# Feature-major products over 256 and 384 token columns instead of 386 and 256, with the padding columns put in where products leave PSUM

## The chip, the cores and the metric

The kernel runs on one core of a Trainium2 chip. The metric is the device time of one execution in microseconds (us). A core has five engines that run their own instruction streams and meet at semaphores: TensorE (PE, with its weight loads shown apart as PEld), VectorE (DVE), ScalarE (ACT), GpSimd (POOL) and SyncE (SP), which here issues all transfers.

## The reference

Two request groups share the weights of two trunk layers: one of 128 context tokens and one of 512 latent tokens. In each layer a combined projection feeds grouped-query attention and a bidirectional state-space scan (SSD); a depthwise convolution over three neighbouring tokens runs on the x, B and C channels and again on the up-projection of the feed-forward part. A convolution must not reach from the last context token into the first latent token, since these are two sequences.

```python
def dw_conv(x, w, b):
    width = w.shape[0]
    pad = width // 2
    xp = jnp.pad(x, ((0, 0), (pad, width - 1 - pad), (0, 0)))
    out = b
    for i in range(width):
        out = out + xp[:, i:i + seq] * w[i]
    return out

def trunk_layer(x, mod, rope, ctx_k, ctx_v, init_state, p):
    h = modulate(x, sh1, sc1)
    proj = h @ p['w_in']
    ...
    attn = block_attention(q, k_all, v_all)
    xbc = jax.nn.silu(dw_conv(xbc, p['conv_w'], p['conv_b']))
    ssd, h_final = ssd_branch(xbc, z, dt_raw, ...)
    merged = jax.nn.sigmoid(ga) * (attn @ p['w_attn_o']) + jax.nn.sigmoid(gs) * (ssd @ p['w_ssd_o'])
    x = x + g1 * (merged @ p['w_out'])
    h = modulate(x, sh2, sc2)
    u = dw_conv(h @ p['w_up'], p['ffn_conv_w'], p['ffn_conv_b'])
    u_val, u_gate = jnp.split(u, 2, axis=-1)
    x = x + g2 * ((jax.nn.silu(u_gate) * u_val) @ p['w_down'])
```

## The kernel before

**Tokens.** The 640 tokens are five tiles of 128: tile 0 is the context, tiles 1 to 4 are the latent grid. Every fp32 product is made of three matmuls on values rounded to a short form and their remainders: high by high, high by low, low by high.

**Two kinds of product.** A token-major product (`tok_major`) holds a token tile as weights and moves 512 columns of a weight matrix; 24 matmuls make one. A feature-major product (`feat_half`) holds 128 weight columns and moves tokens, which the convolution wants along the free dimension. It is done in two parts `h` of 24 matmuls each. The normalised tokens `hT` (and `h2` after the second norm) lie in four tiles, high and low for each part, in the buffers `slab0` and `slab1`.

**Padding before.** Two columns of zeros stand between the context and the latent tokens already in `hT`: `new_hT` has GpSimd set them to zero, so that part 0 has 386 columns (tiles 0 to 2 and the padding) and part 1 has 256 (tiles 3 and 4). The products carry the zeros along, and `conv_in` copies each part out of PSUM as one run of columns: once plainly into `raw`, once times the middle tap plus the bias into `cc`. `conv_taps` then adds the left and right neighbours over 642 columns. There are 69 feature-major products of two parts in each layer: 16 for x, 8 for B and C, one for dt, 44 for the up-projection.

**Order.** Nothing is issued as it is written. `Flow` records all operations with what they read and write, and a list scheduler orders them with its own costs and its own count of free buffers; each engine's program is that order. A buffer class hands its buffers out in the order in which they were asked for. The first product of `up_item` in each layer runs its part 0 for four feature tiles and then its part 1 for the four; all later ones alternate the parts. Directly ahead of it stands `w_out_item`, whose last loop normalises the token tiles one after another (`norm_tile`): VectorE adds to the residual, ScalarE sums squares, GpSimd takes the root, VectorE scales, TensorE transposes (eight matmuls against the identity, called T3 for tile 3 and T4 for tile 4 below), ScalarE and VectorE apply shift and scale, and both write the high and the low half into `h2`.

**Tokens waiting in DRAM.** `tok_load` reads attention and SSD outputs back in pieces of four feature tiles, into the same `slab0` and `slab1` buffers.

Of the kernel before, what the change touches and what calls it, by code (L numbers as in the profile page):

```python
# [7 lines left out]
F32 = mybir.dt.float32  # L8
# [10 lines left out]
P = 128  # L19
# [5 lines left out]
HALF = (386, 256)  # L25
HOFF = (0, 386)
# [14 lines left out]
def _mask(dims, cache={}):  # L41
    """Bits of the free elements that an access pattern touches."""
    m = cache.get(dims)
    if m is None:
        m = 1
        for s, n in reversed(dims):
            if s == 0 or n == 1:
                continue
            if m == 1 and s == 1:
                m = (1 << n) - 1  # L50
            else:
                b = 0
                for i in range(n):
                    b |= m << (s * i)
                m = b
        cache[dims] = m
    return m
# [22 lines left out]
class Flow:  # L80
    """Records the program as operations on tiles, orders them with a list scheduler (dependences by the
    elements touched, buffers granted in the order in which they were asked for) and issues them in that order."""
# [259 lines left out]
def hybrid_step_kernel(  # L342
# [159 lines left out]
    # token-major product: stationary tokens, moving weights of 512 columns  # L502
# [16 lines left out]
    # tokens in two parts: tiles 0 to 2 and tiles 3 and 4  # L519
    def part(i):  # L520
        return (0, col(i)) if i < 3 else (1, col(i) - HOFF[1])

# [4 lines left out]
    # tokens that wait in DRAM: two quads of feature tiles, in pieces of four, tile after tile  # L527
    def tok_load(src, q0):
        pieces = []
        tiles = []  # L530

        def load(n):
            for _ in range(n):
                i = len(tiles)
                while len(pieces) < 4 * i + 4:
                    h, k = (0, 6) if len(pieces) < 12 else (1, 4)
                    t = slab(h, [P, k, 4, P], F32R)
                    pieces.extend(t[:, j] for j in range(k))
                for r in range(2):
                    t = t2((P, 4, P))  # L540
                    dma.dma_start(t.rearrange("p k t -> p (k t)"), src[q0 + r, i])
                    split(pieces[4 * i + 2 * r], pieces[4 * i + 2 * r + 1], t)
                tiles.append(lambda a, kt, i=i: pieces[4 * i + 2 * (kt // 4) + a][:, kt % 4, :])

        return tiles, load

    # feature-major product: stationary weights of 128 columns, moving tokens
# [12 lines left out]
    def new_hT():  # L560
        res = []
        for _ in range(2):
            pair = [slab(h, [P, 8, HALF[h]], F32R) for h in range(2)]
            pool.memset(pair[0][:, :, P:P + 2].bitcast(F32), 0.0)
            res.append(pair)
        return res
# [5 lines left out]
    def norm_x(xh, xns, junk):  # L572
        """Both halves of a token tile over their root mean square."""
# [28 lines left out]
    def norm_tile(x0, x1, t, i, modT, hT):  # L602
        """x0 and t are written over."""
# [11 lines left out]
    def mw():  # L615
        """Of its own while attention holds the other buffers."""
        return t2() if flow.cls == "m" else flow.tile(tmp, [P, 512], F32, "mw", nm("mw"), 1)
# [34 lines left out]
    # the first shifts and scales, straight to features on partitions: columns of silu(cond) in two parts  # L652
    def mod_T_first(ws):
# [3 lines left out]
        for n in range(2):  # L657
            for m in range(2):
# [15 lines left out]
                # the two parts and the bias  # L674
# [30 lines left out]
    def conv_bufs():  # L705
        raw, cc = cv()[:, 0:COLS + 2], cv()[:, 0:COLS]
        pool.memset(raw[:, 0:1], 0.0)
        pool.memset(raw[:, COLS + 1:COLS + 2], 0.0)
        return raw, cc

    def conv_in(raw, cc, ps, h, w1, b):
        o = HOFF[h]
        act.activation(cc[:, o:o + HALF[h]], ps, AF.Identity, scale=w1, bias=b)
        act.copy(raw[:, 1 + o:1 + o + HALF[h]], ps)

# [11 lines left out]
    def later(fn):  # L727
        """Record what was put off last, put this off in its stead."""
# [11 lines left out]
    # ================= the program as a list of items =================  # L740
# [59 lines left out]
    def layer(l):  # L800
# [13 lines left out]
        def qk_normed(ps, n0, nh, t, a):  # L814
            """RMS norm per head, then rotary (t >= 1) or plain weights (t == 0); token-major."""
# [84 lines left out]
        def attn_gen(g):  # L900
            kT, V = S["kT"], S["V"]
            qT, qc = S["qT", g], S["qc", g]
            # context tokens
# [56 lines left out]
        def dt_item(ws):  # L960
            raw = cv()
            for h in range(2):
                ps = feat_half(ws[0], P, 0, S["hT"], h)
                act.activation(raw[0:64, HOFF[h]:HOFF[h] + HALF[h]], ps[0:64, :], AF.Identity, bias=S["dtb"])
# [69 lines left out]
        def to_tok(cc, dst):  # L1034
            """feature-major padded [128, 642] -> token-major [128 tok, 5, 128 feat]"""
# [71 lines left out]
        def ssd_gen(g):  # L1107
# [23 lines left out]
            # C over B, and B by tokens behind it, in two parts  # L1131
# [23 lines left out]
            # context states leave as they are  # L1155
# [429 lines left out]
```

## Time and profile before

| | us |
|---|---|
| three timed runs | 2855.76, 2860.41, 2860.75 |
| their median | 2860.41 |
| span of the profiled execution, first to last instruction | 2854.8 |
| TensorE busy in that span | 2816.5 |
| VectorE, ScalarE, GpSimd busy | 2066.4, 1291.9, 90.5 |

The profiled execution is listed by its span alone; its own time with what lies around the span is not among the runs, of which the fastest is 1.0 us and the median 5.6 us above the span. The trace puts all operations on one source line (the recording helper), so they are told apart by tiles and shapes. A matmul's listed duration holds its pipeline as well; what it costs in a dense stream is the distance from its start to the start of the next.

### The profile page before, as it was taken

The numbers are of one execution on the slowest core, as the hardware profiler recorded it, in microseconds if no ns is written. First come the engines' busy times: TensorE is split into PE (matmuls) and PEld (weight loads), VectorE is DVE, ScalarE is ACT, GpSimd is POOL, SyncE is SP. The second block draws the span as 40 slices with busy tenths as digits, with TensorE's granted clock in tenths as the row PEclk, the third lists the DMA queues.
The fourth block names the chain that finished last, engine by engine and source line by source line (L and its number), as shares of the span: only waits on it lengthen the run. The fifth ranks groups of instructions, "written<-read, shape, count | busy, mean of one in ns | idle before, by whom it ended". The sixth has DMA issues, their size and how long they took to land.

```text
span 2854.8 us, 41191 instructions
## 1 busy us (share of the span) xinstructions
PE 2816.5 (99%) x15620; PEld 2456.6 (86%) x15620; DVE 2066.4 (72%) x2851; ACT 1291.9 (45%) x2255; POOL 90.5 (3%) x408
## 2 busy tenths in 40 slices
PE   6999999999999999999999999999999999999999
PEld 4898997877788898998979989887887888989898
DVE  7878775987799599997677666598779456545554
ACT  6454654445353453452444645544454325524342
POOL 1200000000000000000011000000000000000000
PEclk9999999999999999999999999999999999999999
DMA  7343444677868546455352223457667553252423
GB/s 262 100 125 126 126 151 143 225 247 245 275 219 275 180 136 215 167 175 180 98 168 85 94 95 100 155 199 251 220 235 258 203 175 132 86 166 65 155 84 111
DMA packets 309679, 478.45 MB, mean 168 GB/s; under 512 B 19808, under 2 KB 139792, under 8 KB 304360
## 3 DMA queue, kind: packets, MB, share of 16 engines
q1 hardware_dynamic: 309480, 475.81, 50.0%
q8 instruction: 123, 2.02, 0.3%
q14 instruction: 76, 0.62, 0.1%
HBM read 384.08 MB, written 91.65 MB: 167 GB/s over the span
## 4 chain that ended last, share of the span: by engine, by line
PE 95%; DMA 3%; DVE 1%; ACT 1%; issue 0%; SPq 0%; POOL 0%; DVEq 0%; ACTq 0%
PE pf L178 79%; PE p L178 10%; PE pp L178 4%; PE pq L178 1%; DMA tmp<-in_state_ssd_dram 1%; DMA slab<-in_w_mod_dram 0%; DVE tmp L178 0%; DMA ga<-tmp 0%; DVE wl L178 0%; DMA tmp<-in_x_prompt_dram 0%; ACT tmp L178 0%; SPq L178 0%; DMA slab<-in_q_norm_dram 0%; DVE slab L178 0%; ACT wh L178 0%
## 5 line engine op out<-in xcount | busy, mean ns | idle before, releaser
L178 PE MATMUL pf<-wh,slab 128*128 128x512 f32 x3920 | 1268.3, 400 | 5.9 <-ACT slab L178 2.5
L178 PE MATMUL pf<-slab,wh 128*128 128x256 f32 (+1 forms) x4416 | 980.2, 311 | 3.4 <-DVE slab L178 1.9
L178 PEld LDWEIGHTS pf<-wh,slab 128*128 128x128 f32 x3920 | 733.1, 189 | 174.4 <-issue 7.3
L178 PE MATMUL pf<-wl,slab 128*128 128x512 f32 x1960 | 780.7, 398 | 0.0
L178 PEld LDWEIGHTS pf<-slab,wh 128*128 128x128 f32 x4416 | 741.8, 189 | 12.0 <-issue 5.7
L178 PE MATMUL pf<-slab,wl 128*128 128x256 f32 (+1 forms) x2208 | 685.1, 310 | 0.0
L178 DVE TENSOR_TENSOR wl<-wr,wh 128x2048 fp32r<-128x2048 f32 (+1 forms) x156 | 350.7, 2248 | 145.3 <-ACT wh L178 144.5
L178 PEld LDWEIGHTS pf<-wl,slab 128*128 128x128 f32 x1960 | 369.5, 189 | 86.6 <-issue 6.0
L178 ACT CAST wh<-wr 128x2048 fp32r<-128x2048 f32 (+1 forms) x156 | 293.0, 1879 | 320.7 <-PE pf L178 302.4
L178 PEld LDWEIGHTS pf<-slab,wl 128*128 128x128 f32 x2208 | 415.9, 188 | 3.0 <-issue 0.2
L178 DVE SCALAR_TENSOR_TENSOR tmp<-tmp,fw,tmp 128x642 f32<-128x642 f32 x176 | 155.5, 885 | 80.5 <-ACT tmp L178 66.3
L178 PE MATMUL p<-tmp,slab 128*128 128x64 f32 (+1 forms) x976 | 209.8, 336 | 0.3 <-DVE tmp L178 0.3
L178 ACT ACTIVATE tmp<-tmp 128x642 f32<-128x642 f32 (+2 forms) x176 | 120.9, 687 | 179.1 <-DVE tmp L178 145.5
L178 ACT ACTIVATE tmp<-pf,fw 128x386 f32<-128x386 f32 (+1 forms) x176 | 109.0, 620 | 175.4 <-PE pf L178 172.2
L178 DVE TENSOR_TENSOR tmp<-pf,tmp 128x512 f32<-128x512 f32 x100 | 68.3, 688 | 132.1 <-PE pf L178 131.8
L178 PEld LDWEIGHTS p<-tmp,slab 128*128 128x128 f32 x976 | 136.0, 190 | 16.2 <-ACT tmp L178 4.6
L178 ACT COPY tmp<-pf 128x256 f32<-128x256 f32 (+3 forms) x296 | 127.5, 431 | 44.1 <-PE pf L178 43.7
L178 DVE TENSOR_TENSOR slab<-tmp,slab 128x512 fp32r<-128x512 f32 (+4 forms) x182 | 109.0, 634 | 42.9 <-ACT slab L178 42.7
L178 DVE SCALAR_TENSOR_TENSOR macc<-tmp,cT,macc 128x512 f32<-128x512 f32 x196 | 137.7, 743 | 1.2 <-DMA tmp<-in_w_mod_dram 1.2
L178 DVE TENSOR_TENSOR tmp<-tmp,tmp 128x512 f32<-128x512 f32 (+3 forms) x190 | 133.7, 705 | 3.0 <-DMA tmp<-sz 0.6
L178 PEld LDWEIGHTS p<-cst,tmp 128*128 128x128 f32 (+2 forms) x750 | 92.3, 141 | 40.6 <-issue 16.1
L178 PE MATMUL p<-cst,tmp 128*128 128x128 f32 (+2 forms) x750 | 121.0, 276 | 5.1 <-DMA tmp<-in_state_ssd_dram 4.4
(131 smaller groups left out, 2564.3 us busy)
## 6 DMA issues: line engine op xcount, KB each, us to landing
wr<-in_w_in_dram SPq DMA_DIRECT2D x60, 1024.0 KB
wr<-in_w_up_dram SPq DMA_DIRECT2D x44, 1024.0 KB
slab<-row SPq DMA_DIRECT2D x40, 1024.0 KB
tmp<-in_w_mod_dram SPq DMA_DIRECT2D x116, 256.0 KB
tmp<-xres SPq DMA_DIRECT2D x85, 256.0 KB
wr<-in_w_down_dram SPq DMA_DIRECT2D x20, 1024.0 KB
tmp<-xs SPq DMA_DIRECT2D x72, 256.0 KB
xres<-tmp SPq DMA_DIRECT2D x70, 256.0 KB
```

What stands on the lines that cost most here:

```text
L178: self.ops.append((lane, lambda: call(*args, **kw), self._cost(lane, fn, outs, ins, kw), deps, touched, self.cls))
```

## The change

Part 0 becomes tiles 0 and 1 (256 columns) and part 1 tiles 2, 3 and 4 (384 columns); `hT` has no padding. `conv_in` writes a part out of PSUM tile-wise through a view (`padded`) that leaves the two padding columns out, and `conv_bufs` has GpSimd set these two columns to zero in `raw` and in `cc`. `dt_item` writes through the same view. `tok_load` follows the new sizes: the first two tiles of a quad lie in `slab0`, the other three in `slab1`. Comments were taken out as well.

```diff
-HALF = (386, 256)
-HOFF = (0, 386)
+HALF = (256, 384)
...
     def part(i):
-        return (0, col(i)) if i < 3 else (1, col(i) - HOFF[1])
+        return (0, i * P) if i < 2 else (1, (i - 2) * P)
+
+    def padded(t, b, o=0):
+
+        if b == 0:
+            return t[:, o:o + 2 * P + 4].rearrange("p (a t) -> p a t", a=2)[:, :, 0:P]
+        return t[:, o + col(2):o + COLS].rearrange("p (a t) -> p a t", a=3)
...
-                    h, k = (0, 6) if len(pieces) < 12 else (1, 4)
+                    h, k = (0, 4) if len(pieces) < 8 else (1, 6)
...
     def new_hT():
         res = []
         for _ in range(2):
-            pair = [slab(h, [P, 8, HALF[h]], F32R) for h in range(2)]
-            pool.memset(pair[0][:, :, P:P + 2].bitcast(F32), 0.0)
-            res.append(pair)
+            res.append([slab(h, [P, 8, HALF[h]], F32R) for h in range(2)])
         return res
...
     def conv_bufs():
         raw, cc = cv()[:, 0:COLS + 2], cv()[:, 0:COLS]
         pool.memset(raw[:, 0:1], 0.0)
+        pool.memset(raw[:, P + 1:P + 3], 0.0)
+        pool.memset(cc[:, P:P + 2], 0.0)
         pool.memset(raw[:, COLS + 1:COLS + 2], 0.0)
         return raw, cc
 
     def conv_in(raw, cc, ps, h, w1, b):
-        o = HOFF[h]
-        act.activation(cc[:, o:o + HALF[h]], ps, AF.Identity, scale=w1, bias=b)
-        act.copy(raw[:, 1 + o:1 + o + HALF[h]], ps)
+        ps = ps.rearrange("p (a t) -> p a t", t=P)
+        act.activation(padded(cc, h), ps, AF.Identity, scale=w1, bias=b)
+        act.copy(padded(raw, h, 1), ps)
...
-                act.activation(raw[0:64, HOFF[h]:HOFF[h] + HALF[h]], ps[0:64, :], AF.Identity, bias=S["dtb"])
+                act.activation(
+                    padded(raw[0:64], h), ps[0:64].rearrange("p (a t) -> p a t", t=P), AF.Identity, bias=S["dtb"]
+                )
```

The change also moves instructions, through the scheduler. The first place is TensorE where `w_out_item` of the second layer ends and the up-projection begins; `pf_3689` is the last product of `w_out`, `pf_3709` and `pf_3712` are the first two up products, `slab_3653` and `slab_3655` the high and low half of part 0 of `h2`. Before:

```order
L178 MATMUL pf_3689<-wh_3646,slab_3562 128x512
L178 MATMUL pf_3689<-wl_3647,slab_3560 128x512
L178 MATMUL pf_3709<-slab_3653,wh_3649 128x386
L178 MATMUL pf_3712<-slab_3653,wh_3698 128x386
L178 MATMUL pf_3709<-slab_3655,wh_3649 128x386
L178 MATMUL pf_3709<-slab_3653,wl_3650 128x386
```

and with the change:

```order
L177 MATMUL pf_3689<-wh_3646,slab_3562 128x512
L177 MATMUL pf_3689<-wl_3647,slab_3560 128x512
L177 MATMUL pf_3709<-slab_3653,wh_3649 128x256
L177 MATMUL pf_3709<-slab_3655,wh_3649 128x256
L177 MATMUL pf_3709<-slab_3653,wl_3650 128x256
L177 MATMUL pf_3709<-slab_3653,wh_3649 128x256
```

The second up product's first matmul no longer stands between a high and a low matmul of the first one. Some hundred rows further, the transposes of tile 4 (T4, `p_3591` and `p_3592`) and the first matmul of part 1 (`pf_3719`, from `slab_3654` and `slab_3656`) stand in the changed kernel as follows, with 95 matmuls of 256 columns between the end of `w_out` and T4:

```order
L177 MATMUL pf_3718<-slab_3653,wh_3698 128x256
L177 MATMUL pf_3718<-slab_3655,wh_3698 128x256
L177 MATMUL p_3591_3695<-cst_84,tmp_3692 128x128 x4
L177 MATMUL p_3592_3696<-cst_84,tmp_3691 128x128 x4
L177 MATMUL pf_3718<-slab_3653,wl_3699 128x256
L177 MATMUL pf_3719<-slab_3654,wh_3649 128x384
L177 MATMUL pf_3719<-slab_3656,wh_3649 128x384
```

Before, T4 stood earlier in the part, inside the third product, and 45 matmuls of part 0 followed it:

```order
L178 MATMUL pf_3715<-slab_3653,wl_3650 128x386
L178 MATMUL p_3591_3695<-cst_84,tmp_3692 128x128 x4
L178 MATMUL p_3592_3696<-cst_84,tmp_3691 128x128 x4
L178 MATMUL pf_3715<-slab_3653,wh_3649 128x386
L178 MATMUL pf_3715<-slab_3655,wh_3649 128x386
```

The second place is ScalarE in the same stretch: `tmp_3707` and `tmp_3708` are `raw` and `cc` of the first up product, `tmp_3684` and `slab_3654` belong to tile 3, `tmp_3692`, `tmp_3691` and `sm_3693` to tile 4. Before:

```order
L178 CAST wh_3701<-wr_3700 128x2048
L178 ACTIVATE tmp_3684<-p_3583_3687,sm_3627 128x128 x4
L178 CAST slab_3654<-tmp_3684 128x4x128
L178 ACTIVATE tmp_3708<-pf_3709,fw_2252 128x386
L178 ACTIVATE tmp_3691,sm_3693<-tmp_3692 128x512
L178 COPY tmp_3707<-pf_3709 128x386
L178 ACTIVATE tmp_3691,sm_3693<-tmp_3690 128x512
```

and with the change:

```order
L177 CAST wh_3701<-wr_3700 128x2048
L177 COPY tmp_3707<-pf_3709 128x2x128
L177 ACTIVATE tmp_3708<-pf_3709,fw_2252 128x2x128
L177 ACTIVATE tmp_3684<-p_3583_3687,sm_3627 128x128 x4
L177 CAST slab_3654<-tmp_3684 128x4x128
L177 ACTIVATE tmp_3691,sm_3693<-tmp_3692 128x512
L177 COPY tmp_3710<-pf_3712 128x2x128
L177 ACTIVATE tmp_3691,sm_3693<-tmp_3690 128x512
```

Both copies of the first up product now stand ahead of tile 3's shift and scale, and a copy of the second one stands between the two sums of squares of tile 4.

## Rows read from the trace of the kernel before

**Rows 1.** The page, part 1: busy time and share of each engine.
```profile
PE 2816.5 (99%) x15620; PEld 2456.6 (86%) x15620; DVE 2066.4 (72%) x2851; ACT 1291.9 (45%) x2255; POOL 90.5 (3%) x408
```

**Rows 2.** Waits of TensorE: us in total, times, longest.
```profile
PE p L178 <- DMA tmp<-in_state_ssd_dram: 4.4, 5, 1.4
...
PE pf L178 <- ACT slab L178: 3.9, 4, 1.6
PE pf L178 <- DVE slab L178: 3.9, 4, 1.7
```

**Rows 3.** Groups by shape, TensorE: count, then busy us and mean ns.
```profile
L178 PE MATMUL pf<-slab,wh 128*128 128x386 f32 x2208 | 585.3, 343 | 3.4 <-DVE slab L178 1.9 <-ACT slab L178 1.5
...
L178 PE MATMUL pf<-slab,wl 128*128 128x386 f32 x1104 | 377.0, 341 | 0.0
```

**Rows 4.** Timeline of TensorE, up-projection of layer 2: start, duration (us).
```profile
2466.20 0.52 PE L178 MATMUL pf<-slab,wh 128*128 128x386 f32 x2
...
2470.46 0.40 PE L178 MATMUL pf<-slab,wh 128*128 128x256 f32 x2
...
2473.19 0.52 PE L178 MATMUL pf<-slab,wh 128*128 128x386 f32 x2
```

**Rows 5.** Timeline of TensorE inside `w_out` of layer 2.
```profile
2374.54 0.64 PE L178 MATMUL pf<-wh,slab 128*128 128x512 f32 x2
...
2380.10 0.62 PE L178 MATMUL pf<-wh,slab 128*128 128x512 f32 x2
```

**Rows 6.** Timeline of TensorE in attention, layer 1.
```profile
160.38 1.04 PE L178 MATMUL pp<-slab,slab 128*128 128x320 f32 x6
161.26 0.33 PE L178 MATMUL pf<-slab,wh 128*128 128x386 f32 x1
```

**Rows 7.** Timeline of TensorE, `w_out` to up-projection, layer 2; idle in brackets.
```profile
2383.51 0.39 PE L178 MATMUL pf<-wl,slab 128*128 128x512 f32 x1
2384.64 0.59 PE L178 MATMUL pf<-slab,wh 128*128 128x386 f32 x2 [0.74 <-ACT slab L178]
2386.18 0.42 PE L178 MATMUL pf<-slab,wh 128*128 128x386 f32 x1 [0.94 <-DVE slab L178]
...
2389.20 1.43 PE L178 MATMUL p<-cst,tmp 128*128 128x128 f32 x8
...
2397.55 1.06 PE L178 MATMUL p<-cst,tmp 128*128 128x128 f32 x8
```

**Rows 8.** Timeline of TensorE at the same place in layer 1.
```profile
979.80 0.59 PE L178 MATMUL pf<-slab,wh 128*128 128x386 f32 x2 [0.73 <-ACT slab L178]
981.34 0.41 PE L178 MATMUL pf<-slab,wh 128*128 128x386 f32 x1 [0.95 <-DVE slab L178]
...
983.34 1.09 PE L178 MATMUL p<-cst,tmp 128*128 128x128 f32 x8
```

**Rows 9.** Windows: stretch, length, busy us by engine, PEclk, DMA share.
```profile
978.00:981.50 3.50, 1.81 (x8) 1.04 (x7) 3.50 (x5) 3.50 (x9) 0.63 (x1) 1.00 0.03 13
...
2386.60:2390.40 3.80, 3.80 (x18) 3.70 (x17) 3.40 (x6) 1.01 (x2) 0.90 (x5) 0.55 0.96 341
```

**Rows 10.** Timeline of VectorE, layer 2: scaling of tile 3, a weight remainder.
```profile
2387.63 0.89 DVE L178 TENSOR_SCALAR tmp<-tmp,sm 128x512 f32<-128x512 f32 x2 [0.40 <-POOL sm L178]
...
2389.03 2.29 DVE L178 TENSOR_TENSOR wl<-wr,wh 128x2048 fp32r<-128x2048 f32 x1
```

**Rows 11.** Timeline of ScalarE, layer 2: shift and scale, then high halves.
```profile
2398.21 1.51 ACT L178 ACTIVATE tmp<-p,sm 128x128 f32<-128x128 f32 x4
2399.76 1.14 ACT L178 CAST slab<-tmp 128x512 fp32r<-128x512 f32 x2
```

**Rows 12.** Timeline of VectorE, layer 2: low halves of tile 4.
```profile
2400.41 1.29 DVE L178 TENSOR_TENSOR slab<-tmp,slab 128x512 fp32r<-128x512 f32 x2 [0.39 <-ACT slab L178]
```

**Rows 13.** Groups by shape, ScalarE's scaled copy of 256 columns, GpSimd memsets.
```profile
L178 ACT ACTIVATE tmp<-pf,fw 128x256 f32<-128x256 f32 x88 | 49.6, 564 | 53.2 <-PE pf L178 53.2
...
L178 POOL MEMSET tmp<- 128x1 f32 x272 | 18.1, 107 | 1156.0 <-DVE tmp L178 766.0 <-DMA xs<-tmp 83.3 <-DMA xres<-tmp 82.8
```

## The prediction

> **What bounds the kernel now.** The page's first part comes first: TensorE is busy for 2816.5 of 2854.8 us, no other engine for more than 72% [rows 1]. Then the waits of TensorE: the reader should see how short the list is. The waits for SSD states, for the high halves (ScalarE) and for the low halves (VectorE) of feature-major operands come to 4.4, 3.9 and 3.9 us [rows 2]; half of the latter two are the two places where `w_out` hands over to the up-projection [rows 7, 8]. So the time is the number of TensorE's matmuls times their distance in a dense stream, plus a few us of stalls. What frees ScalarE, VectorE or GpSimd is worth nothing by itself; what shortens a matmul counts in full, what makes TensorE wait counts too.
>
> **The distance of matmuls.** The listed durations of some 340 ns [rows 3] hold the pipeline, so distances are read from starts. One part of 386 columns takes from 2466.20 to 2470.46 us for 24 matmuls, 177.5 ns each, and the following part of 256 columns to 2473.19, 113.8 ns each [rows 4]. In `w_out` 24 matmuls of 512 columns take 5.56 us, 231.7 ns each [rows 5]; in attention six of 320 take 0.88 us, 146.7 ns each [rows 6].
>
> **The two columns.** The change makes no matmul fewer; it makes 386 columns into 384 in 2208 + 1104 = 3312 matmuls [rows 3]. No row shows 384 columns. From 256 to 386 a column costs 63.7/130 = 0.49 ns, from 386 to 512 it costs 54.2/126 = 0.43 ns. Two columns are then 0.86 to 0.98 ns; I take 0.92, and 3312 x 0.92 ns = **3.0 us**. The upper bound comes from straight lines that leave 386 out, in case it is an awkward size. Between 320 and 512 a column costs 85.0/192 = 0.443 ns, so 384 would take 146.7 + 28.3 = 175.0 ns, 2.5 ns less than 386: 8.3 us in all. Between 256 and 512 it would take 113.8 + 128 x 0.461 = 172.7 ns, 4.8 ns less: 15.9 us. A loss I exclude, since fewer columns are streamed from the same buffers. I take the low end, because 386 is the nearest row, and because 320, which is as round as 384, also lies above the line from 256 to 512 (143.3 ns there, 146.7 measured).
>
> **The hand-over to the up-projection.** Here the change moves a wait, and this needs a chain of its own for each layer.
>
> Before, part 0 needs tile 2, the third of five. In layer 2 the last `w_out` matmul starts at 2383.51, so a dense stream would go on at 2383.74; the first high matmul starts at 2384.64 and the first low one two matmuls later, at 2386.18, 1.18 us later than it might. That is 2.0 us lost [rows 7], and the same in layer 1 [rows 8]. In layer 2 the granted clock then falls to 0.55 for 3.8 us, mostly its lower level, 1.2 GHz [rows 9], and T3 takes 1.43 us where it took 1.09 in layer 1 [rows 7, 8]. From 2386.6 to T3 at 2389.20 eight matmuls start, about 320 ns apart; against 177.5 this loses 1.2 us, with T3 1.5 us. So this place costs 2.0 us in layer 1 and 3.5 us in layer 2: **5.5 us**.
>
> After, part 0 needs tiles 0 and 1 alone, which are long done; both stalls go. What is late next is tile 4, since part 1 now needs tiles 2 to 4, and four parts of 256 columns cover less than four of 386 did. In layer 2: T3 stands 38 matmuls behind 2383.74, at 2388.1, and its operand is scaled from 2387.63 on, half of it in 0.45 us [rows 10]: 0.1 us of waiting at most. T4 comes after 95 matmuls (10.8 us) and T3 (0.9): 2395.4. Its operand hangs on ScalarE, where the copies of the first product, at most 0.57 us each [rows 13], now stand ahead of tile 3's shift and scale, and where a copy of the second product stands between tile 4's two sums of squares. That copy waits for a buffer which VectorE frees with tile 3's first low half, after a weight remainder that ends at 2391.3 [rows 10], so about 2392.2. I reckon the squares end at 2393.5, the root and the scaling's first half at 2395.8 (estimate by the same steps before): 0.4 us of waiting. From T4's start to tile 4's first high half it took from 2397.55 to 2400.3, to its first low half until 2401.05, that is 2.8 and 3.5 us [rows 7, 11, 12], while T4 and the one matmul behind it fill 1.0 us. TensorE waits 1.9 us, runs one high matmul and waits 0.5 more. Sum: about 2.9 us, and the chance of one in two (one of the two gaps of 2 us did it) of the same clock loss of 1.5 us: 3.6, against 3.5 before. In layer 1 six matmuls of the modulation fill part of the gap once T4's PSUM tile is read; I reckon 1.5 us there against 2.0. Net gain **0.5 us**, bounds: both stalls vanish (5.5 us gained), or both are 2 us longer than reckoned and the clock falls twice (about 6 us lost).
>
> The Trainium skill's page TensorE: Matmul & The Clock Gate, section What's actually happening, says that the monitor's window runs free and doesn't start with the kernel; so the same gap may cost clock in one place and not in another. The trace agrees: of two equal gaps only one was followed by a clock of 0.55 [rows 9]. By this rule the repeated runs of one kernel differ at such a place too.
>
> **The memsets.** GpSimd gets 272 memsets of two columns and loses eight on `hT`: 264 x 107 ns [rows 13] is 28 us on an engine busy for 90.5 [rows 1], and none is on TensorE's chain in the up-projection, where `conv_taps` starts a whole part later. Were the cover gone, VectorE would start its taps 0.1 to 0.4 us later per product, and with a busy share of 72% it takes that up. The Trainium skill's page SBUF — State Buffer, section Who interferes with whom, speaks against them: GpSimd and VectorE share a port pair, and a VectorE operation in a two-port mode blocks or is blocked in full while the other runs. The page counts tensor_scalar among these, which scales the tiles here. At each hand-over some seven of these memsets lie near tile 4's chain; at 107 ns each [rows 13] that would be 0.7 us twice, and the gain of the hand-over would turn into a loss of 0.9 us. No row shows such a block, so the sum leaves it out and the range holds it.
>
> **What else moves.** ScalarE copies the same columns in parts of 256 and 384; a strided write could cost it more, and it is busy for 45% [rows 1]. The token quads come back one tile later into `slab1`: a tile that was split during three later products (3 x 5.56 us [rows 5]) now has two, 11 us, for two casts and two subtractions of 0.57 and 0.65 us [rows 11, 12]. Hidden. The order of attention and SSD between the feature-major products shifts by a product here and there; TensorE waits there for states in five places [rows 2], and this may go either way by 1 to 2 us.
>
> **Sum.** 2854.8 - 3.0 - 0.5 = 2851.3 us of span. Against the median of the runs shown, 5.6 us above the span of the profiled execution: 2860.4 - 3.5 = **2856.9 us**, 0.12% faster. About 0.2%, 5.7 us, is what a measurement of this kernel can tell from no change.
>
> **Rivals.**
> 1. *384 is a better size than the neighbour shows.* For it: 386 lies 1.7 to 4.8 ns above the lines through rounder sizes. Against it: 320 lies above the line from 256 too. It gives 8.3 + 0.5 = 8.8 us, 2851.6 us, and as far as 2844 by the other line.
> 2. *The hand-over eats the gain.* Part 1 waits for tile 4 as reckoned and the clock falls in both layers: stalls of 2.9 + 1.5 + 2 x 1.5 = 7.4 us against 5.5. With the columns: -3.0 + 1.9, 2859.3 us. For it: the gap is again over 2 us long. Against it: in layer 1 other matmuls split it.
> 3. *Slower: the states come late.* The new order in SSD brings the transposes of the states ahead of their transfers. There are sixteen such loads (two layers, four groups, two directions); five wait now, up to 1.4 us [rows 2]. Eleven more at 1.4 us are 15.4 us: 2872.3 us. It decides, that is ends over 0.2% slower, from seven more at 1.4 us (9.8 against 3.5 gained). Against it: five of sixteen wait now, and the program moves by a product at most places.
>
> **Chances.** The likeliest, two columns at the price of their neighbours and waits that trade places: 0.58, with its own range of 2852 to 2861 (hand-over 3 us either way, runs scattering). Rival 1: 0.20. Rival 2: 0.12. Rival 3: 0.08. Something else: 0.02. The range that leaves out the far ends of rivals 1 and 3 is 2849 to 2864 us. Faster by over 0.2%: a fifth of the likeliest and most of rival 1, 0.29. Slower: rival 3 and little else, 0.08. Within: 0.63.
>
> **What would show it.** In the profile after: 24 matmuls of 384 columns take 4.24 us (176.6 ns each) where rival 1 has 4.20 or less; those of 256 stay at 113.8. At the end of `w_out` TensorE goes straight into 256-column matmuls, in both layers, and the bracketed waits for ScalarE and VectorE stand at the first 384-column product behind T4, of about 1.9 and 0.5 us in layer 2. The waits for states stay near 4 us. The prediction is wrong if 384 columns take under 175 ns, if the wait behind T4 is over 4 us or gone, or if a new wait shows in attention or SSD.

## The result and the profile after

| | us |
|---|---|
| four timed runs of the changed kernel | 2880.12 to 2881.49 |
| their median | 2880.43 |
| median of the kernel before | 2860.45 |
| ratio, with its 95% interval | 1.0081 (1.0067 to 1.0095) |
| span of the profiled execution | 2879.7 |

The changed kernel is 0.8% slower; 2856.9 us was predicted. The profiled executions differ by 24.9 us, since that of before lies at the lower end of its runs; against the medians 20 us are to be explained.

The page of the changed kernel, part 1, answers to [rows 1]: the same number of matmuls, 9.5 us more busy time of TensorE, and so some 15 us more in which it doesn't run.

```profile
PE 2826.0 (98%) x15620; PEld 2459.2 (85%) x15620; DVE 2067.5 (72%) x2851; ACT 1293.1 (45%) x2255; POOL 110.4 (4%) x672
```

The waits of TensorE (us in total, times, longest) answer to [rows 2]. The waits for states went down, and a wait for a VectorE result that had a row of 1.5 us before leads the list.

```profile
PE pf L177 <- DVE tmp L177: 12.2, 3, 10.5
...
PE p L177 <- DMA tmp<-in_state_ssd_dram: 1.6, 1, 1.6
```

Where that is, the stages tell. In each layer the z and gate products are followed by the attention's output product (`attn_o`), by that of the SSD in two halves of its channels (`ssd_oA` and `ssd_oB`, ten products each) and by `w_out`. Last matmuls of each stage of layer 1 against before: gates 0.9 us earlier, `ssd_oA` 862.04 against 859.97, `ssd_oB` 943.43 against 919.05. So 22 of the 24.9 us come up between the ends of `ssd_oA` and `ssd_oB` of layer 1, and after that the two kernels stay 20 to 26 us apart to the end. The timeline of TensorE there, with idle time in brackets:

```profile
867.88 0.72 PE L177 MATMUL pp<-tmp,slab 128*128 128x512 f32 x2
...
880.32 1.67 PE L177 MATMUL p<-tmp,slab 128*128 128x64 f32 x14
...
887.68 0.39 PE L177 MATMUL pf<-wl,slab 128*128 128x512 f32 x1
898.57 1.22 PE L177 MATMUL pf<-wh,slab 128*128 128x512 f32 x2 [10.50 <-DVE tmp L177]
```

The `pp` and 64-column matmuls are the SSD's last two token tiles; before, they stood ahead of the end of `ssd_oA`, and from 860 us on TensorE ran nothing but products and transposes. Now they are late: `ssd_oB` needs the SSD's output, and when the few products that can run without its last tile are done, TensorE has nothing left. The same stretch in windows (busy us by engine, then PEclk, DMA share, GB/s) shows VectorE full while TensorE is empty, and the granted clock at 0.63, that is mostly at its lower level of 1.2 GHz. From 898.5 to 905 us it is 0.66, which costs some 2 us more (an estimate, 6.5 x 0.34):

```profile
890.00:900.00 10.00, 1.44 (x3) 1.16 (x4) 10.00 (x17) 0.62 (x1) 0.00 (x0) 0.63 0.92 322
```

The 22 us are not all waiting. Between these two ends TensorE is idle for 11.2 us in gaps of over 150 ns, where it had none before; its products take 2.7 us longer, 10.2 us of the stretch being at the lower clock; and 8.3 us are matmuls of the SSD and transposes that had been done by then before. So the nearly equal ends of `ssd_oA` hide some 10 us (8.3 + 2.1) that TensorE had lost already: up to there its gaps come to 29.8 us against 25.7, and the clock was at the lower level for 17.1 us against 10.2.

What the last tile waits for stands in SyncE's queue and on VectorE. `y<-tmp` stores an SSD output tile and `tmp<-y` brings it back; of eight loads of modulation weights six are queued ahead of the last store and two between it and its return:

```profile
884.49 2.90 SPq L177 DMA_DIRECT2D tmp<-in_w_mod_dram  x6
887.49 0.60 SPq L177 DMA_DIRECT2D y<-tmp  x1
890.05 1.65 SPq L177 DMA_DIRECT2D tmp<-in_w_mod_dram  x2
893.47 0.33 SPq L177 DMA_DIRECT2D tmp<-y  x1
```

and on VectorE the modulation sums stand ahead of the tile's low half and of the addition that empties a PSUM buffer (`tmp<-pf,tmp`):

```profile
889.94 7.37 DVE L177 SCALAR_TENSOR_TENSOR macc<-tmp,cT,macc 128x512 f32<-128x512 f32 x11
897.23 0.68 DVE L177 TENSOR_TENSOR slab<-tmp,slab 128x512 fp32r<-128x512 f32 x1
897.83 0.68 DVE L177 TENSOR_TENSOR tmp<-pf,tmp 128x512 f32<-128x512 f32 x1
```

Before, the last store was this one, 29 us earlier and 1.6 us ahead of the last matmul of `ssd_oA`:

```profile
858.34 0.38 SPq L178 DMA_DIRECT2D y<-tmp  x1
```

The lag has a history. The products up to `ssd_oA` end within 6 us of where they ended before, but attention's last store goes from 452.95 to 471.57 us, the first SSD store from 529.39 to 544.19, the eleventh from 707.35 to 737.83. In layer 2 the SSD is some 26 to 37 us later than before too, of which 24 are layer 1's; there its last store, at 2247.28, is 42 us ahead of the end of `ssd_oA`, so it costs nothing.

**Distances.** In the up-projection of layer 2, 24 matmuls of 256 columns now take 2.83 us, 117.9 ns each, and 24 of 384 take 4.16 us, 173.3 ns each; it was 113.8 for 256 and 177.5 for 386 [rows 4]:

```profile
2756.05 0.40 PE L177 MATMUL pf<-slab,wh 128*128 128x256 f32 x2
...
2758.88 0.51 PE L177 MATMUL pf<-slab,wh 128*128 128x384 f32 x2
...
2763.04 0.40 PE L177 MATMUL pf<-slab,wh 128*128 128x256 f32 x2
```

The two parts together take what they took, 6.99 us. For the accounts below I use means over all starts of a trace (start to next start inside the products, gaps left out):

| ns from start to start | before | changed |
|---|---|---|
| 386 / 384 columns, up-projection (2112 matmuls) | 177.4 | 173.3 |
| 386 / 384 columns, x, B, C and dt (1200) | 177.1 | 173.4 |
| 256 columns, up-projection (2112) | 113.7 | 117.7 |
| 256 columns, x, B, C and dt (1200) | 116.7 | 117.4 |
| 512 columns, all token-major products (5880) | 231.8 | 232.8 |

That is 8.5 + 4.5 = 13.0 us less, 8.3 + 0.8 = 9.1 us more and 6.0 us more: a dense stream that is 2.1 us longer. The 512-column rise has a place: products whose weights are token tiles from `slab0` and `slab1` (k, v, q, z, gates, `attn_o`, `ssd_oA`, `ssd_oB`: 85 of them in each layer, 4080 matmuls in all) go from 231.5 to 233.1, while `w_out` and the down-projection, with weights from other buffers, stay between 231 and 232.5.

**The hand-over** in layer 2 [rows 7]: TensorE goes straight from `w_out` into part 0 at 2408.33, and waits behind tile 4's transposes instead.

```profile
2420.47 1.04 PE L177 MATMUL p<-cst,tmp 128*128 128x128 f32 x8
...
2423.31 0.44 PE L177 MATMUL pf<-slab,wh 128*128 128x384 f32 x1 [1.69 <-ACT slab L177]
...
2424.04 0.45 PE L177 MATMUL pf<-slab,wh 128*128 128x384 f32 x1 [0.29 <-DVE slab L177]
```

Behind these waits the granted clock falls in layer 2 as it did before: it is 0.63 from 2424.0 to 2428.6 us, mostly the lower level; in layer 1 it stays at 1.00. From the end of `w_out` to the end of the up-projection the changed kernel gains 1.5 us on before in layer 1 and nothing in layer 2.

### The profile page after: what moved, and what is told of

Same layout as the page of the kernel before. It is cut to its first block, busy times and chain, and to the rows that moved or that the text cites. A ratio compares the mean times of both kernels' runs of the same rounds, so it can differ in the third digit from the quotient of the medians.

```text
span 2879.7 us, 41481 instructions
## 1 busy us (share of the span) xinstructions
PE 2826.0 (98%) x15620; PEld 2459.2 (85%) x15620; DVE 2067.5 (72%) x2851; ACT 1293.1 (45%) x2255; POOL 110.4 (4%) x672
## 4 chain that ended last, share of the span: by engine, by line
PE 95%; DMA 2%; DVE 1%; ACT 1%; issue 1%; SPq 0%; POOL 0%; DVEq 0%; ACTq 0%; POOLq 0%
PE pf L177 79%; PE p L177 10%; PE pp L177 4%; PE pq L177 1%; ACT tmp L177 1%; DVE tmp L177 1%; DMA slab<-in_w_mod_dram 0%; DMA tmp<-in_x_prompt_dram 0%; DMA tmp<-in_state_ssd_dram 0%; DVE wl L177 0%; DMA slab<-row 0%; DVE slab L177 0%; SPq L177 0%; DMA slab<-in_q_norm_dram 0%; POOL sm L177 0%
## 5 line engine op out<-in xcount | busy, mean ns | idle before, releaser
L177 PE MATMUL pf<-slab,wh 128*128 128x384 f32 (+1 forms) x4416 | 980.0, 310 | 2.3 <-ACT slab L177 1.7
L177 PE MATMUL pf<-slab,wl 128*128 128x384 f32 (+1 forms) x2208 | 684.7, 310 | 0.0
L177 ACT ACTIVATE tmp<-pf,fw 128x384 f32<-128x384 f32 (+1 forms) x176 | 108.9, 619 | 177.1 <-PE pf L177 168.9
L177 ACT COPY tmp<-pf 128x384 f32<-128x384 f32 (+3 forms) x296 | 127.5, 431 | 36.7 <-PE pf L177 35.0
L177 DVE SCALAR_TENSOR_TENSOR tmp<-tmp,tmp 128x642 f32<-128x642 f32 (+2 forms) x130 | 98.2, 757 | 42.8 <-ACT tmp L177 41.9
L177 ACT CAST slab<-tmp 128x512 fp32r<-128x512 f32 (+2 forms) x146 | 91.6, 650 | 74.0 <-DVE tmp L177 42.6
```

The costliest lines, as they stand in the source:

```text
L177: self.ops.append((lane, lambda: call(*args, **kw), self._cost(lane, fn, outs, ins, kw), deps, touched, self.cls))
```

## Experiments

**Is it the order, or the parts themselves?** Four kernels. Two are the kernel before with one number of its scheduler changed, two are the changed kernel. First:

```diff
-                    heapq.heappush(slots[x.tag], x.end + 150.0)
+                    heapq.heappush(slots[x.tag], x.end + 151.0)
```

> The kernel before with one number of its scheduler changed: a buffer is reckoned free 151 ns after its last use instead of 150. The same operations on the same tiles; only the order in which they stand can differ. In that order the SSD's last output tile of layer 1 stands about five 512-column products later beside the products. Theory A (the loss of the change is the order: SSD work falls behind the products, and at the end of ssd_oA in layer 1 TensorE has no product left): the last store of an SSD output tile in layer 1 goes from 858 us to about 880 to 888, TensorE waits 8 to 12 us between ssd_oA and ssd_oB, and the time is 2872 to 2884 us. Theory B (the parts of 256 and 384 columns, their copies or their loads cost the time wherever they stand): 2860 us, plus or minus 3, since none of them is in this kernel.

Measured: 2872.97 us (before, on the same chip: 2858.54), ratio 1.0051 (1.0036 to 1.0066). The last store is at 878.37, and TensorE waits at the same place, without a single part regrouped. Its products are 6.4 us earlier than before at the end of `ssd_oA` and 14.9 us later at the end of `ssd_oB`:

```profile
889.77 1.22 PE L178 MATMUL pf<-wh,slab 128*128 128x512 f32 x2 [10.11 <-DVE tmp L178]
```

The same line with 152.0:

> The kernel before with the same number at 152 ns. The order differs from that of before too, but the SSD's last tile of layer 1 stands as early as before. Theory A: last store at 858 us plus or minus 4, no wait of over 2 us between ssd_oA and ssd_oB, 2857 to 2864 us. Theory B: the same, 2860 us. A rival to theory A, that any disturbance of an order that was picked out costs some 20 us, expects 2870 us or more here.

Measured: 2859.11 us, ratio 0.9999 (0.9990 to 1.0009); last store at 858.25. So it isn't that any nudge costs: of 150, 151 and 152 only 151 does.

Third, the changed kernel with another price of a matmul:

```diff
-                return max(n, 256) / 2.4 + 2 if n > 128 else 213.0
+                return max(n, 256) / 2.4 + 4 if n > 128 else 213.0
```

> The changed kernel, its scheduler reckoning a matmul at its columns at full clock plus 4 ns instead of 2. The operations are those of the changed kernel; in their order the SSD's last tile of layer 1 stands before the end of ssd_oA, as it did before the change. Theory A: no wait of over 3 us between ssd_oA and ssd_oB, the whole 24 us of that stretch come back but for 2 or 3: 2855 to 2862 us. Theory B: only the wait itself goes (10.5 us and some 2.5 us of lower clock behind it), and the rest stays: 2866 us or more.

Measured: 2869.58 us, ratio 1.0046 (1.0030 to 1.0063): by its number that is theory B. The trace speaks for A in this stretch: last store at 853.17, no wait, and at the end of `ssd_oB` of layer 1 the kernel is level with before (919.09 against 919.05). Its 11 us are lost in layer 2, from the gates on, where this order has a new wait in `attn_o`, with the lower clock around it:

```profile
2156.12 1.19 PE L177 MATMUL pf<-wh,slab 128*128 128x512 f32 x2 [3.17 <-DVE tmp L177]
```

Fourth, the side work in front of the tile is held back:

```diff
+                    if i == 3 and n == 0:
+                        S["oB"].append(len(flow.ops) - 1)
...
+                if held:
+                    flow.hold = held[0]
...
-            mod_item(0, 10)
-            mod_item(0, 11)
+            mod_item(0, 10, S["oB"])
+            mod_item(0, 11, S["oB"])
```

> The changed kernel with the loads of the last two modulation chunks of layer 1 held back until the fourth product of ssd_oB, so that neither their eight loads nor VectorE's 13 operations on them stand between the last SSD tile's store and its return; nothing else is recorded differently. Theory A1 (of the 10.5 us of waiting most is this side work in front of the tile): the wait falls to 3 to 5 us, and the time to 2870 to 2875 us. Theory A2 (the wall is the tile's own way out to memory and back, and the side work fills a gap that is there anyway): the wait stays at 8 us or more, 2877 to 2882 us.

Measured: 2880.19 us, ratio 1.0073 (1.0058 to 1.0088). In the profiled execution the wait falls to 5.35 us and its span is 2872.0, as A1 has it, but the other three runs (2880 to 2882 us) don't show it. With the loads out of the way half the wait is gone in that execution; what that is worth in time stays unclear.

```profile
891.35 1.22 PE L177 MATMUL pf<-wh,slab 128*128 128x512 f32 x2 [5.35 <-DVE tmp L177]
```

**Why do 256 and 512 columns get slower?** The buffers' sizes changed with the parts: 12352 bytes a partition for part 0 and 8192 for part 1 before, 8192 and 12288 now. With the first at byte 143936, the four buffers stood at offsets 64, 128, 192, 192 within 256 bytes before, and all stand at 64 now; the weight buffers `wh` and `wl` are at 0 in both. The changed kernel with sizes 64 bytes up, which makes the offsets 64, 128, 192, 0:

```diff
-        return flow.tile(slabs, shape, dt, f"slab{h}", nm("slab"), 2)
+        n = int(np.prod(shape[1:]))
+        t = flow.tile(slabs, [P, (2048, 3072)[h] + (16, 16)[h]], dt, f"slab{h}", nm("slab"), 2)[:, 0:n]
...
```

> The changed kernel with 64 unused bytes behind each of the four token buffers in every partition; order and operations are the same. In the changed kernel the four buffers start 8192 or 12288 bytes apart, all at the same offset within 256 bytes; before, one was 12352 long and they started at three different ones. Seen so far: 512-column products whose weights come from these buffers are 233.2 ns apart in the changed kernel and 231.5 before, in all three changed kernels and all three of before, while w_out and down, whose weights come from other buffers, did not move. Theory C (the buffers' places make it): the 4080 matmuls of 512 columns go back to about 231.5, 7 us less, 2873 us; where the 256-column distance goes back too, from 117.7 to 113.7, another 9 to 13 us less, 2862 us. Theory D (it comes with the parts or the order): distances as they are, 2879 to 2882 us.

Measured: 2880.85 us, ratio 1.0073 (1.0056 to 1.0091). The distances moved with the order as it was: 512 columns 232.8 to 231.2 in the mean (230.8 on the token buffers), but 384 columns up to 175.3 in the up-projection, 256 almost unmoved at 117.2. That is some 5 us less in the sum, which the runs don't show: theory C has the 512 columns right and the time wrong. The reverse, the kernel before with `slab0` at 12544 bytes, all offsets 64:

```diff
-        return flow.tile(slabs, shape, dt, f"slab{h}", nm("slab"), 2)
+        n = int(np.prod(shape[1:]))
+        t = flow.tile(slabs, [P, (3136, 2048)[h]], dt, f"slab{h}", nm("slab"), 2)[:, 0:n]
...
```

> The kernel before with the first two token buffers 192 bytes longer, so that all four start at the same offset within 256 bytes, as they do in the changed kernel; order and operations are those of before. Theory C: the 512-column products from these buffers go from 231.5 to about 233 ns, and the time up by some 6 us (2865 us); Theory D: nothing moves, 2857 to 2861 us.

Measured: 2872.09 us, ratio 1.0049 (1.0030 to 1.0068), with every engine's order as it was. 256 columns go from 113.7 to 117.9 in the up-projection, 512 to 232.8, and 386 hardly move, from 177.4 to 176.8:

```profile
2780.26 0.40 PE L178 MATMUL pf<-slab,wh 128*128 128x256 f32 x2
...
2783.09 0.52 PE L178 MATMUL pf<-slab,wh 128*128 128x386 f32 x2
...
2787.34 0.40 PE L178 MATMUL pf<-slab,wh 128*128 128x256 f32 x2
```

Theory C was short here: I had expected only the 512 columns to move. So moved buffers alone can make both rises of the change, and with all four at 64, 384 columns are 3.5 ns shorter than 386.

Which buffers' place counts is not shown by this. The scratch buffers (`tmp`, which hold `raw` and `cc` too, and the small ones) lie behind the token buffers, so each of these edits moved them along. The four token buffers come to 41088 bytes before and 40960 in the changed kernel, 41216 in `a_pad64` and 41472 in `b_pad192`: a multiple of 256 in the last three, 128 more in the first. In the up-projection 256 columns take 117.2 to 117.9 ns in these three and 113.7 in the first, and the runs that follow keep to this split: 117.5 in `a_order_mix` with 41216 bytes, 113.5 in some stretches of `a_off192` and `a_order_off192` with 41088, the unused tiles counted in. So for the 256 columns the place of the scratch buffers is a rival that no run here takes apart from the token buffers' own. For the 512 columns the token buffers' places do count: the changed kernel and `a_pad64` have the scratch buffers at one offset within 256 bytes, at 233.1 and 230.8 ns.

**Another order, and both together.** VectorE takes SSD and attention by record order:

```diff
-        "pe": {"m": 0, "d": 1, "f": 2}, "act": {"f": 0, "d": 1, "m": 2}, "dve": {"f": 0, "d": 1, "m": 2},
+        "pe": {"m": 0, "d": 1, "f": 2}, "act": {"f": 0, "d": 1, "m": 2}, "dve": {"f": 0, "d": 0, "m": 2},
```

> The changed kernel with one rank of its scheduler changed: on VectorE, SSD and attention no longer stand behind the products' own work when both are ready; the one recorded first goes first. The same operations; the SSD's last tile of layer 1 stands well ahead of the end of ssd_oA. Theory A: no wait of over 3 us between ssd_oA and ssd_oB in layer 1, and that stretch back to where it was; with some us lost elsewhere, since the products' own work on VectorE now waits at times: 2857 to 2866 us. Theory B (the parts cost it wherever they stand): 2867 us or more, with layer 1 still 10 us behind the kernel before at its w_out.

Measured: 2873.64 us, ratio 1.0050 (1.0033 to 1.0066). A miss for theory A: the number is theory B's, and layer 1 is 13 us behind before at its `w_out`. The trace has another place for it: `ssd_oA` to `ssd_oB` is even with before, but 24 us go in the z products of layer 1 and only a part of them comes back. So the two other orders tried on the changed kernel are without the wait but lose time elsewhere, and theory B still stands.

> The two last together on the changed kernel: the rank on VectorE and the 64 bytes. If A and C both hold, the gains add: 7 us below the run with the rank alone, 2850 to 2859 us, the first that may beat the kernel before. If C fails: the same as with the rank alone.

Measured: 2870.60 us, ratio 1.0041 (1.0026 to 1.0056): 3 us below the last, within the intervals of both. Then offset 192 for all four buffers, by an unused tile of 128 bytes ahead of them:

```diff
+        if not gap:
+            gap.append(slabs.tile([P, 32], F32, tag="gap", name="gap", bufs=1))
...
```

> The changed kernel with 128 unused bytes ahead of the four token buffers, so that all four start at offset 192 within 256 bytes instead of 64; order and operations are the same. Before, the two buffers of the 256-column part lay at 192 and gave 113.7 ns; at 64, in the run with the longer buffers of before, they gave 117.9. Theory C (the place sets the distance): 256 columns fall from 117.7 to about 113.7 in the up-projection (2112 matmuls, 8.4 us), 512 columns from 233.1 to 231.5 or less (4080 matmuls, 6.5 us), 384 stay at 173.3: 2862 to 2869 us, or up to 2875 where waits take back some of it, as they did with 64 bytes between the buffers. If only the equal offsets of the four count, not which: distances as they are, 2879 to 2882 us.

Measured: 2869.41 us, ratio 1.0039 (1.0024 to 1.0054): 11 us below the changed kernel with the same order, and with the wait still in it. 512 columns fall to 229.6 on the token buffers; 256 fall to 115.8 in the mean and not 113.7, and 384 rise to 174.6. These two means are mixtures: the up-projection of layer 2 falls into three stretches, with parts of the down-projection between them, and 256 and 384 columns take 117.8 and 176.7 ns in the first (from 2435 us), 113.5 and 173.2 in the second (from 2575) and 117.7 and 174.8 in the third (from 2741), all from the same buffers. Next, an order chosen so that the SSD stands as early as before in both layers:

```diff
-                return max(n, 256) / 2.4 + 2 if n > 128 else 213.0
+                return max(n, 256) / 2.4 + 4.5 if n > 128 else 213.0
...
-        "dma": {"pe": 1200.0, "act": 1200.0, "dve": 1200.0, "pool": 1200.0, "dma": 1500.0},
+        "dma": {"pe": 1300.0, "act": 1300.0, "dve": 1300.0, "pool": 1200.0, "dma": 1500.0},
...
-                hw = max(hw, tb) + 475.0
+                hw = max(hw, tb) + 520.0
...
-                    heapq.heappush(slots[x.tag], x.end + 150.0)
+                    heapq.heappush(slots[x.tag], x.end + 140.0)
```

> The changed kernel with four numbers of its scheduler changed (4.5 ns beside a matmul's columns instead of 2, a buffer free after 140 ns instead of 150, 520 ns between transfers instead of 475, 1300 ns of latency instead of 1200); operations and buffers are the same. In this order the SSD stands beside the products as early as before the change, in both layers. Theory A: the wait between ssd_oA and ssd_oB is gone, and the time is that of the kernel before plus what the distances cost, 2857 to 2864 us. Theory B: 2868 us or more, as in the two orders tried so far.

Measured: 2860.28 us, ratio 1.0007 (0.9998 to 1.0017). The whole 20 us are back (ratio 1.0081 to 1.0007) with the parts, copies, memsets and places of the changed kernel in it; the last SSD store of layer 1 stands in SyncE's queue three us ahead of that of before:

```profile
855.47 0.33 SPq L177 DMA_DIRECT2D y<-tmp  x1
```

Theory B falls. Both together:

> The order of the last run and the places of the one ahead of it together. If both theories hold, the gains add and 384 columns at 173.3 ns beside 256 at 113.7 are left as what the change itself is worth: 13 us below the kernel before in distances, 2842 to 2850 us. If the places give nothing in this order, as the last run.

Measured: 2846.42 us, ratio 0.9958 (0.9943 to 0.9973), 0.4% faster than the kernel before. The number is in the range, but not by the distances expected. Against `a_order` the gain of 13.9 us is nearly all in the 512 columns (232.8 to 230.4 in the mean over 5880 matmuls, 14 us); 256 gain 2.5 and 384 lose 1.1 ns in the up-projection, again as mixtures.

**The memsets.** The kernel before with the two new memsets of `conv_bufs` added:

```diff
+        pool.memset(raw[:, P + 1:P + 3], 0.0)
+        pool.memset(cc[:, P:P + 2], 0.0)
```

> The kernel before with the two memsets of the changed kernel in each pair of convolution buffers beside those that it has, 264 more; nothing else. Hidden, as the prediction has it: 2857 to 2861 us. If GpSimd's memsets hold up VectorE (28 us of them, 107 ns each), it shows as longer operations of VectorE near them and 2864 us or more.

Measured: 2857.15 us, ratio 0.9994 (0.9985 to 1.0004), with 28.5 us of them on GpSimd (272 and not 264, since `new_hT` keeps its own eight). VectorE's operations don't get longer: it is busy for 2066.3 us against 2066.4, and its 242 tensor_scalar operations take 455 ns in the mean, 456 before:

```profile
L178 POOL MEMSET tmp<- 128x2 f32 x272 | 28.5, 106 | 419.9 <-DVE tmp L178 163.7 <-PE pq L178 158.1 <-issue 40.6
```

**Which edit throws the order, and whose place counts?**

```diff
-HALF = (386, 256)
-HOFF = (0, 386)
+HALF = (258, 384)
+HOFF = (0, 258)
...
-        return (0, col(i)) if i < 3 else (1, col(i) - HOFF[1])
+        return (0, col(i)) if i < 2 else (1, col(i) - HOFF[1])
...
-                    h, k = (0, 6) if len(pieces) < 12 else (1, 4)
+                    h, k = (0, 4) if len(pieces) < 8 else (1, 6)
```

> The kernel before with nothing changed but which tiles a part holds: tiles 0 and 1 with the padding between them (258 columns) in part 0 and tiles 2 to 4 (384) in part 1, token loads to match. The padding stays in the tokens, the copies out of PSUM stay plain, no memset is added. If the regrouping alone throws the order (theory A, narrowed): the last SSD store of layer 1 is 20 us or more late, TensorE waits some 10 us between ssd_oA and ssd_oB, and the time is 2868 to 2880 us. If it takes the padding's move or the memsets to throw it: no such wait, 2856 to 2866 us.

Measured: 2884.13 us, ratio 1.0088 (1.0070 to 1.0106), above the range; its 258 columns take 120.2 ns. The last store is at 885.31, and the wait is there:

```profile
896.29 1.22 PE L178 MATMUL pf<-wh,slab 128*128 128x512 f32 x2 [10.40 <-DVE tmp L178]
```

So the regrouping, with the token loads that follow it, throws the order by itself. Last, `a_order` with unused tiles that put the 256-column part's buffers at 192 and leave those of 384 at 64:

> The changed kernel in the good order, with the two buffers of the 256-column part at offset 192 and those of the 384-column part at 64. If a part's distance hangs on its own buffers' place alone: 256 columns near 113.7 to 115.5 ns, 384 at 173.3, 512 between 230.4 and 232.8; 2842 to 2848 us. If it hangs on how all four lie to each other: 256 stays at 117.5 or 384 at 174.5 or more; 2848 to 2856 us.

Measured: 2854.03 us, ratio 0.9990 (0.9981 to 1.0000). 256 columns stay at 117.5 in the up-projection, 384 at 173.4, 512 are 231.7: the distance of the 256-column part doesn't hang on its own buffers' place alone.

## Why the prediction was wrong

**The step that failed** is the one sentence on the order: "this may go either way by 1 to 2 us", for attention and SSD between the feature-major products. It was worth 20 us (2880.43 against 2860.28 with only the scheduler's numbers changed). I had looked at how far products stood from their old places, and found a few; the lag adds up instead, 15 us by the first SSD store and 29 by the last. What I didn't ask is how much slack the SSD had at its end. Before, the last store came 1.6 us ahead of TensorE's last matmul of `ssd_oA`; with the change it came 25.4 us behind it, and 10.5 us of that were waited for, since the first `ssd_oB` products and the SSD's own last matmuls filled the other 15. `b_release151` (24.8 and 10.1 us) and `b_swap` (25.8 and 10.4) leave the same 15. So the slack was some 17 us, an estimate from these rows, and lag beyond it is paid, with the lower clock on top. `b_release151` shows the wait without any part regrouped, `b_swap` that the regrouping brings it. The wait and the clock there are some 14 us of the loss; the other 10 or so of the profiled execution had been lost in smaller pieces by the end of `ssd_oA`. Which choice of the scheduler flips first was not followed.

**The two columns** were mis-sized: 3.0 us predicted, 13.0 us measured. Rival 1 had the direction (175.0 to 172.7 ns expected, 173.3 measured), and 386 was the awkward size that I named and set aside in favour of the nearest row.

**What stays equal** did not: "those of 256 stay at 113.8" and the 512 columns, which the prediction left untouched, cost 9.1 and 6.0 us. I excluded a loss because fewer columns come "from the same buffers"; they were not in the same places, since the new sizes moved them and the scratch buffers behind them. `b_pad192` shows the rise without the change, 13 us by the runs; whose place makes it for the 256 columns stays open.

**The hand-over** went nearly as worked out: both waits ahead of part 0 gone, 1.69 and 0.29 us behind T4 in layer 2 for 1.9 and 0.5, the lower clock behind them in layer 2, to which the prediction gave one chance in two, and a net gain of 1.5 us for 0.5. In layer 1 TensorE waits 1.04 us there, in front of the modulation's matmuls.

**The memsets** are hidden, as it said (`b_memsets`); the blocked port that the Trainium skill's page SBUF — State Buffer, section Who interferes with whom, describes does not show in that run's time, nor in the length of its tensor_scalar operations.

**The rivals.** Rival 3 had the right side and the wrong place: the waits for states fell from 4.4 to 1.6 us. What came late was the SSD's own output, and its wait stands in one place instead of eleven. Rival 2 did not happen.

The sum in its own terms: order 20, distances 2.1, hand-over 1.5 less, which is 21 against the 20 measured. The distances hide two opposite things, 13 us gained on 384 columns and 15 lost on 256 and 512, a loss that moved buffers can make by themselves (`b_pad192`). With another order and other places the changed kernel is 12 us faster than before (`a_order_off192`); of these some 8 us are 512-column matmuls that lie better than before as well (4080 x 1.9 ns, 229.6 against 231.5), so a like place might speed up the kernel before too. That wasn't tried, nor were orders picked for it as for the changed kernel, so the 12 us are not what the change itself is worth.

## What to carry to other kernels

Where a list scheduler makes the order, ask of every change how much slack each late-running chain has at the point where the next stage needs it, and read that from the trace (last store against the last matmul that can run without it); here some 17 us were left, and the new order came 29 us later. Compare a change with the order held as good as before, by nudging the scheduler's numbers on both sides, before judging the change itself. And when buffers change size, look at where they and the buffers behind them come to lie: 64 bytes behind each of four buffers moved the distance of 4080 matmuls by 2 ns.

## What was not expected of the hardware

The distance of dense matmuls depends on where buffers lie. With the four token buffers all at offset 64 within 256 bytes, 512-column matmuls with weights from them are 233.1 ns apart; at 64, 128, 192, 192 it is 231.5, at 64, 128, 192, 0 it is 230.8, at 192 for all 229.6. That is 3.5 ns or 1.5% between like operations.

256 columns have two distances, about 113.5 and 117.8 ns, and keep to one for whole parts. In the changed kernel the first part of 256 behind a long run of 512-column matmuls, at 2749 us, runs at 113.3 ns, and the next, behind a part of 384, at 117.8, from the same buffers. 384 columns have three, 173.2, 174.8 and 176.7 ns, and `a_off192` shows all three and both of the 256 columns in the up-projection of layer 2, each kept for a whole stretch of up products; in `b_swap` 173.2 and 176.7 alternate from product to product there. So the place is not all of it; something in the course of the run counts too. What it is stays open: the 117.8 ns come behind parts of 384 in the changed kernel, but 113.5 come behind them as well in the second stretch of `a_off192`.
